# Three background matrix-vector blocks per pair of items in the up stages of a two-layer trunk, not four

## The chip, the cores and the metric

The kernel runs as one program on one NeuronCore of a Trainium2 chip. The metric is the device time of one execution in microseconds (us): three runs before the change took 2880.12, 2875.01 and 2872.11 us, median 2875.01. A profiled execution took 2877.94 us. The engines are TensorE (PE, with PEld for its weight loads), VectorE (DVE), ScalarE (ACT), GpSimd (POOL) and SyncE (SP), whose queue issues nearly all DMAs.

## The reference

Two layers, each with a mixer (gated delta net, then retention) and a convolutional feed-forward part. Scales, shifts and gains of both parts come from a conditioning vector `e` by a matrix-vector product with `ada_w`.

```python
e = jax.nn.silu(c @ cond_w + cond_b)
for i in range(DEPTH):
    mod = (e @ ada_w[i] + ada_b[i])[:, None, :]
    sh1, sc1, g1, sh2, sc2, g2 = jnp.split(mod, 6, axis=-1)
    y = mixers[i % N_MIXERS](x * (1.0 + sc1) + sh1)
    x = layer_norm(DN_ALPHA * x + (1.0 + g1) * y, ln_g[i, 0], ln_b[i, 0])
    y = conv_ffn(x * (1.0 + sc2) + sh2, ffn_up[i], ffn_conv_w[i], ffn_conv_b[i], ffn_down[i])
    x = layer_norm(DN_ALPHA * x + (1.0 + g2) * y, ln_g[i, 1], ln_b[i, 1])

def conv_ffn(h, w_up, conv_w, conv_b, w_down):
    gate, up = jnp.split(h @ w_up, 2, axis=-1)
    gate = causal_dwconv(gate, conv_w) + conv_b
    return (jax.nn.silu(gate) * up) @ w_down
```

D is 1024, the sequence 1024, the feed-forward width 2816, all in 32-bit floats; `ada_w` is 2 x 1024 x 6144.

## The kernel before, in words

**Matrix products.** Each operand is split into a high part (a copy by ACT to a reduced type, L89) and a low part (a subtraction by DVE, L90), and each product is three matmuls (L110 to L112, or L301 to L303 in the down projection). PE therefore needs a block's copy, then its low half, before the block's first matmul. The large products use Strassen's scheme in Winograd's form, seven block products in place of eight.

**Up stage** (`strassen`, called at L1781 for the feed-forward part of each layer). It runs 22 items. Items 2fp and 2fp+1 are a pair (`pair_items`): the even one makes 2 x 128 gate columns, the odd one the up columns that belong to them. From item 2 on, each is done by `wino` (L1357): two 512 KB weight loads (L1361, L1362), sums of their halves (`psub`, L1350), seven products, and a `sink` that takes each result. The sink of a gate item adds parts into `g` (L1726); then `conv_q` (L1735 to L1741) runs the convolution on DVE and ends with Silu on ACT. The sink of an up item adds and multiplies (L1762, L1763), stores the result to `ad` in DRAM (L1752), and POOL makes and stores the four combinations that the down projection reads (L1771).

**Background work.** A queue `bg` holds units of the matrix-vector product with `ada_w`. One unit (`bg_ada`) covers 512 columns and 256 rows: it issues one 512 KB load, tile `mvw` (L227, on SP's queue), and at the following step does two products on DVE (L237 or L239). A vector of 1024 columns is eight units, and every fourth unit ends in four transposes on PE (L249) and four copies on ACT. `bg_step` pops the work that is due and issues one new unit. Layer 0's up stage starts with four vectors of layer 1 in the queue (32 units), layer 1's with one (8 units). `wino` calls `bg_step` twice per item, once after the fourth product and once at the end, but not while `late` work is pending at its start (`early`), which holds for items 2 and 3. Units left over when the stage ends stay in the queue; the next loop that calls `bg_step` takes them. The tile that a unit's load goes to is set by `bg_tag[0]`: "lane" (4 buffers) within the up stage, "wr" (2 buffers) after it (L1423).

**Down stage** (`proj_gen`, L1433). Seven products, each over eleven steps j. A step's `ops` (L1482) loads the stationary block (`ar`, from `ad`, L1429), splits it into `ab`, and splits a weight block (`Bw`, `Br`, L1462) into `bb`. The tile of `ab` rotates through ("wl", "hTb", "wr") in the first five products, so that steps 2, 5 and 8 of the first one take a "wr" buffer. Each step ends in `bg_step` (L1651).

**What sets the order.** Instructions of one engine run in the order that a scheduler has given them from the code, its tile pools and its own estimates; each engine's order is fixed when the program is built. A second call of `strassen` serves retention (`direct=True`).

Of the kernel before, what the change touches and what calls it, by code (L numbers as in the profile page):

```python
# [33 lines left out]
def trunk_kernel(ctx: ExitStack, tc, A):  # L34
# [11 lines left out]
    def tl(tag, shape, dt=F32, name=None):  # L46
        return sb.tile(shape, dt, tag=tag, name=name or tag, bufs=BUFS[tag])
# [34 lines left out]
    def hs(half):  # L82
        return slice(half * HALF, (half + 1) * HALF)
# [35 lines left out]
    def bg_step(tile=mm_tile):  # L119
        bg_ps[0] = tile  # L120
        for p in pend:
            p[0] -= 1
        while pend and (pend[0][0] <= 0 or not bg):
            pend.pop(0)[1]()
            if not bg:
                break
        if bg:
            nxt = bg.pop(0)()
            if nxt:
                pend.append(list(nxt))  # L130
# [3 lines left out]
    def row_step():  # L134
        if rowp:
            rowp.pop()()
        if rowq:
            nxt = rowq.pop(0)()
            if nxt:
                rowp.append(nxt[1])  # L140
# [1149 lines left out]
    def strassen(hT0, xts, scale, shift, items, tags=("hTb", "hTb", "qkv", "qkv", "aux"), direct=False, late=()):  # L1290
# [39 lines left out]
        def block(src):  # L1330
            n = nblk[0]
            nblk[0] += 1
            t = tl(("wh", "wl")[n % 2], [P, 2, HALF], F32R, name="wb")
            split(t[:, 0], t[:, 1], src)
            return kn(t[:, 0]), kn(t[:, 1])

        def prod(src, b, onto=None, w=None):
            w = w or block(src)
            if onto is None:
                nacc[0] += 1  # L1340
                acc = (acc_tile, acc_tile, sc_tile)[nacc[0] % 3]()
            else:
                acc = onto
            for k in range(4):
                mm3(acc, w, k, B[b][k], onto is None and k == 0, k == 3, mm_on if onto is not None else pe.matmul)
            return acc

        def psub(x, y, op=ALU.subtract):
            t = mm_tile()
            dve.tensor_tensor(t, x, y, op)  # L1350
            return t

        def drain(n):
            for _ in range(min(n, len(late))):
                late.pop(0)()

        def wino(n, sink):  # L1357
            ua, ub = items[n][:2]
            early = bool(late)
            wa, wb = tl("wr", [P, D]), tl("wr", [P, D])  # L1360
            sp.dma_start(wa, ua)  # L1361
            anchor["wi"] = sp.dma_start(wb, ub)  # L1362
            a11, a12, a21, a22 = wa[:, hs(0)], wa[:, hs(1)], wb[:, hs(0)], wb[:, hs(1)]
            def copy_of(X, tag="cv"):
                t = tl(tag, [P, 516] if tag == "cv" else [P, HALF], name="pc")[:, 0:HALF]
                act.activation(t, X, AF.Copy)  # L1366
                return t

            X = prod(a11, "11")
            p1 = copy_of(X)  # L1370
            s1 = psub(a21, a22, ALU.add)
            sink(0, prod(a12, "21"), p1)
            s2 = psub(s1, a11)
            Z = prod(s1, "T1")
            z5 = copy_of(Z)
            w2 = block(s2)
            s4 = psub(a12, s2)
            drain(2)
            prod(None, "T2", X, w2)
            u2 = copy_of(X)  # L1380
            s3 = psub(a11, a21)
            drain(2)
            prod(s4, "22", Z)
            sink(1, Z, u2)
            if not early:
                bg_step()
            drain(2)
            prod(s3, "T3", X)
            u3 = copy_of(X, "t2")
            sink(3, X, z5)  # L1390
            drain(2)
            sink(2, prod(a22, "T4"), u3)
            if not early:
                bg_step()
            if n > 4:
                row_step()
# [20 lines left out]
        for n in range(2, len(items)):  # L1417
            wino(n, items[n][2]())
            if n > 2:
                drain(len(late))  # L1420
            if items[n][3]:
                items[n][3]()
# [754 lines left out]
```

## Time and profile before

| what | us |
|---|---|
| median of three runs | 2875.01 |
| profiled execution | 2877.94 |
| its span in the trace | 2876.1 |
| up stage of layer 0 (L1296 and L110 to L112) | about 847 to 1164 |
| first matmul of layer 0's down stage (L301) | 1164.69 |
| up stage of layer 1 | about 2300 to 2660 |

The mean granted clock of TensorE is 0.992. The span is the time from the first to the last instruction that the profiler recorded; the profiled time lies 1.8 us above it. A row of the timeline has its start, its length, the engine, the line, the operation and, in brackets, how long the engine stood idle before it and for what.

### The profile page before, as it was taken

Reading aid. Unit: us, or ns where it says so; the run is one execution under the profiler, and the core shown is the slowest. Engines: PE = TensorE matmul, PEld = TensorE weight load, DVE = VectorE, ACT = ScalarE, POOL = GpSimd, SP = SyncE. Lnnn points to the kernel's source line nnn. Section 1 sums busy time; section 2 is a strip of 40 time slices with the busy share of each in tenths; the row PEclk is TensorE's granted clock in tenths of the full one; section 3 lists DMA queues with packets and bytes.
Section 4 is the critical chain, followed back from the end, with each engine's and each line's share of the span. In section 5 each row is a group of like instructions: output and inputs, shape, how many; then the busy total and the mean of one; then the engine's idle time right before and its main releaser. Section 6 shows DMA issues by size and latency. Waiting matters only on the chain.

```text
span 2876.1 us, 38922 instructions
## 1 busy us (share of the span) xinstructions
PE 2787.3 (97%) x13594; PEld 2279.0 (79%) x13594; DVE 2181.4 (76%) x3874; ACT 1296.6 (45%) x2387; POOL 488.7 (17%) x517
## 2 busy tenths in 40 slices
PE   8999999999999999999999999999999999999997
PEld 6788878887787878887888887777777788888886
DVE  5788778676788878778687666666789887777869
ACT  4664465343654444546333332222344644445443
POOL 0311321000023233000000002333301033332001
PEclk9999999999999999999999999999999999999999
DMA  7233232174254655845343364665854153444843
GB/s 278 85 99 122 92 132 96 63 245 147 96 186 159 204 179 176 323 136 181 125 147 113 125 198 157 201 191 173 261 199 148 67 202 133 143 136 163 321 149 117
DMA packets 251988, 465.30 MB, mean 162 GB/s; under 512 B 24144, under 2 KB 76752, under 8 KB 251792
## 3 DMA queue, kind: packets, MB, share of 16 engines
q1 hardware_dynamic: 217472, 407.50, 42.7%
q10 hardware_dynamic: 31488, 46.15, 4.4%
q0 software_dynamic: 2832, 9.18, 0.8%
q8 instruction: 107, 1.75, 0.3%
q14 instruction: 89, 0.73, 0.1%
HBM read 346.86 MB, written 115.87 MB: 161 GB/s over the span
## 4 chain that ended last, share of the span: by engine, by line
PE 64%; DVE 16%; DMA 10%; ACT 5%; issue 4%; POOL 1%; SPq 0%; ACTq 0%; DVEq 0%; POOLq 0%
PE acc L716 10%; PE acc L1296 7%; PE acc L110 5%; PE acc L111 5%; PE acc L112 5%; PE acc L1592 4%; PE sc L716 4%; PE sc L1296 4%; PE mm L716 2%; DMA mvw<-in_ada_w 2%; PE sc L110 2%; PE sc L112 2%; PE sc L111 2%; DVE o L1740 2%; DMA wr<-in_ffn_up 1%
## 5 line engine op out<-in xcount | busy, mean ns | idle before, releaser
L716 PE MATMUL acc<-hT,wh 128*128 128x512 f32 x960 | 299.8, 394 | 0.0
L1592 PE MATMUL acc<-bb,ab 128*128 128x512 f32 x984 | 231.6, 394 | 6.5 <-DVE ab L90 5.3
L89 ACT ACTIVATE ab<-ar 128x512 fp32r<-128x512 f32 x210 | 130.9, 629 | 216.3 <-PE mm L303 56.7
L1592 PEld LDWEIGHTS acc<-bb,ab 128*128 128x128 f32 x984 | 184.0, 189 | 48.9 <-DVE ab L90 4.6
L716 PEld LDWEIGHTS acc<-hT,wh 128*128 128x128 f32 x960 | 182.3, 190 | 35.6
L1296 PE MATMUL acc<-T,wb 128*128 128x512 f32 x840 | 202.0, 389 | 0.4 <-DVE wb L90 0.4
L89 ACT ACTIVATE wb<-mm 128x512 fp32r<-128x512 f32 x216 | 124.3, 597 | 170.6 <-DVE mm L1350 155.3
L90 DVE TENSOR_TENSOR ab<-ar,ab 128x512 fp32r<-128x512 f32 x210 | 148.0, 712 | 69.6 <-ACT ab L89 68.9
L716 PE MATMUL acc<-hT,wl 128*128 128x512 f32 x480 | 196.6, 410 | 2.1 <-ACT sq L509 2.1
L1296 PEld LDWEIGHTS acc<-T,wb 128*128 128x128 f32 x840 | 157.5, 188 | 33.8 <-ACT o L1741 1.2
L90 DVE TENSOR_TENSOR wl<-wr,wh 128x1024 fp32r<-128x1024 f32 x98 | 121.4, 1239 | 76.6 <-ACT wh L89 72.7
L90 DVE TENSOR_TENSOR wb<-wr,wb 128x512 fp32r<-128x512 f32 x162 | 116.2, 719 | 65.8 <-ACT wb L89 65.7
L89 ACT ACTIVATE wh<-wr 128x1024 fp32r<-128x1024 f32 x98 | 103.8, 1060 | 127.9 <-PE acc L716 59.6
L1771 POOL TENSOR_TENSOR o<-o 128x512 f32<-128x512 f32 x80 | 113.0, 1421 | 268.6 <-DVE o L1763 130.8
L1740 DVE SCALAR_TENSOR_TENSOR o<-g,vc,o 128x512 f32<-128x512 f32 (+2 forms) x176 | 147.3, 846 | 7.1 <-ACT o L1735 5.9
L90 DVE TENSOR_TENSOR wb<-mm,wb 128x512 fp32r<-128x512 f32 x216 | 144.4, 680 | 7.3 <-ACT wb L89 7.3
L89 ACT ACTIVATE wb<-wr 128x512 fp32r<-128x512 f32 x162 | 101.2, 626 | 91.8 <-PE acc L1296 26.5
L1350 DVE TENSOR_TENSOR mm<-wr 128x512 f32<-128x512 f32 x108 | 84.9, 786 | 73.1 <-DMA wr<-in_ffn_up 59.8
L716 PE MATMUL acc<-wh,hT 128*128 128x512 f32 x384 | 134.3, 412 | 1.8 <-DVE vv L90 1.8
L1366 ACT ACTIVATE pc<-acc 128x512 f32<-128x512 f32 x143 | 84.4, 590 | 110.7 <-PE acc L1296 63.9
L239 DVE SCALAR_TENSOR_TENSOR ada<-mvw,e,ada 128x512 f32<-128x512 f32 x140 | 105.3, 752 | 24.5 <-DMA mvw<-in_ada_w 24.2
L110 PE MATMUL acc<-T,wb 128*128 128x512 f32 x292 | 114.4, 392 | 4.6 <-DVE wb L90 4.6
(677 smaller groups left out, 7350.9 us busy)
## 6 DMA issues: line engine op xcount, KB each, us to landing
wr<-in_ffn_up SPq DMA_DIRECT2D x92, 512.0 KB, 3.9
mvw<-in_ada_w SPq DMA_DIRECT2D x80, 512.0 KB, 4.3
ad<-o SPq DMA_DIRECT2D x154, 256.0 KB, 2.3
ar<-ad SPq DMA_DIRECT2D x154, 256.0 KB, 4.6
Br<-in_ffn_down SPq DMA_DIRECT2D x88, 256.0 KB, 5.2
wr<-in_ret_wv SPq DMA_DIRECT2D x32, 512.0 KB, 3.7
ar<-od SPq DMA_DIRECT2D x56, 256.0 KB, 4.2
wr<-in_gdn_wqkv SPq DMA_DIRECT2D x24, 512.0 KB, 3.5
```

Source lines behind the costliest of these rows:

```text
L89: anchor["sp"] = act.activation(dst_h, src, AF.Copy)
L90: eng.tensor_tensor(dst_l, src, dst_h, ALU.subtract)
L110: mm(acc, wl[:, k], hl[0], start=first, stop=False)
L111: mm(acc, wh[:, k], hl[1], start=False, stop=False)
L112: mm(acc, wh[:, k], hl[0], start=False, stop=last)
L239: dve.scalar_tensor_tensor(a, wr[:, kk], e[:, k:k + 1], a, ALU.mult, ALU.add)
L716: pq(pe.matmul(out, lhsT, rhs, start=start, stop=stop), cost or COST[out.shape[-1]])
L1296: return pe.matmul(*a, skip_group_check=True, **kw)
L1350: dve.tensor_tensor(t, x, y, op)
L1592: return pe.matmul(*args, skip_group_check=True, **kw)
L1740: dve.scalar_tensor_tensor(tv, gv[:, c0 - j:c1 - j], w[:, 2 - j:3 - j], tv, ALU.mult, ALU.add)
L1771: (dve if fp == 0 else pool).tensor_tensor(o[d], o[x], o[y], op)
```

## The change

The first of the two calls of `bg_step` in `wino` is now made only in items with an even number (those with gate columns), and in the retention call as before. The second one, at the item's end, stays.

```diff
             prod(s4, "22", Z)
             sink(1, Z, u2)
-            if not early:
+            if not early and (n % 2 == 0 or direct):
                 bg_step()
             drain(2)
             prod(s3, "T3", X)
...
             sink(2, prod(a22, "T4"), u3)
             if not early:
                 bg_step()
```

For items 4 to 21 of an up stage this is 27 steps, not 36. In layer 0 the queue of 32 units is then not empty at the stage's end: five are issued by the steps of the down stage.

The rows of DVE (line, operation, output and inputs) in the up item of pair 8/9 of layer 0's up stage, before; `ada<-mvw` are a unit's two products, L1350 the sums of weight halves, the first of them needing the second weight load:

```order
L90 TENSOR_TENSOR wb<-wr,wb 128x512 x2
L1350 TENSOR_TENSOR mm<-wr 128x512
L253 SCALAR_TENSOR_TENSOR v_8007<-cs,vc 128x4
L237 TENSOR_SCALAR ada<-mvw,e 128x512
L1350 TENSOR_TENSOR mm<-mm,wr 128x512
L274 TENSOR_TENSOR fs_12000<-v_8007,vc 128x8
L275 TENSOR_TENSOR fh_12001<-v_8007,vc 128x8
L1726 TENSOR_TENSOR g<-acc,pc 128x512
L239 SCALAR_TENSOR_TENSOR ada<-mvw,e,ada 128x512
L90 TENSOR_TENSOR wb<-wr,wb 128x512
L1740 SCALAR_TENSOR_TENSOR o<-g,vc,o 128x512 x2
```

and now:

```order
L1740 SCALAR_TENSOR_TENSOR o<-g,vc,o 128x511
L239 SCALAR_TENSOR_TENSOR ada<-mvw,e,ada 128x512
L1740 SCALAR_TENSOR_TENSOR o<-g,vc,o 128x510
L239 SCALAR_TENSOR_TENSOR ada<-mvw,e,ada 128x512
L90 TENSOR_TENSOR wb<-wr,wb 128x512 x2
L1726 TENSOR_TENSOR g<-acc,pc 128x512
L1350 TENSOR_TENSOR mm<-wr 128x512
L90 TENSOR_TENSOR wb<-wr,wb 128x512
L1350 TENSOR_TENSOR mm<-mm,wr 128x512
L1740 SCALAR_TENSOR_TENSOR o<-g,vc,o 128x512 x2
```

The two products have moved from behind the first L1350 to ahead of it.

SP's queue at the end of layer 0's up stage, before (names with their numbers; `ad0` is the store of gated columns, `ar` its reload, `Bw` the weights):

```order
L1462 DMA Bw_10628<-in_ffn_down 128x512 x2
L1462 DMA Bw_10631<-in_ffn_down 128x512
L1752 DMA ad0_6815<-o_10456 128x512
L1429 DMA ar_10637<-ad0_6815 128x512
L1462 DMA Bw_10631<-in_ffn_down 128x512
L1429 DMA ar_10658<-ad0_6815 128x512
```

and now, with a second piece from a few rows later, where the third and the fourth of the five units stand:

```order
L1462 DMA Bw_10582<-in_ffn_down 128x512 x2
L1462 DMA Bw_10585<-in_ffn_down 128x512
L227 DMA mvw_10614<-in_ada_w 128x2x512
L1752 DMA ad0_6815<-o_10406 128x512
L227 DMA mvw_10652<-in_ada_w 128x2x512
L1429 DMA ar_10591<-ad0_6815 128x512
L1462 DMA Bw_10585<-in_ffn_down 128x512
L1429 DMA ar_10616<-ad0_6815 128x512
```

```order
L1429 DMA ar_10831<-ad0_6815 128x512
L1462 DMA Br_10839<-in_ffn_down 128x512
L1752 DMA ad0_6815<-o_10421 128x512
L227 DMA mvw_10678<-in_ada_w 128x2x512
L1429 DMA ar_10841<-ad0_6815 128x512
L1462 DMA Br_10849<-in_ffn_down 128x512
L227 DMA mvw_10704<-in_ada_w 128x2x512
L1429 DMA ar_10883<-ad0_6815 128x512
```

Four of the five loads now stand between the stores and reloads with which the down stage begins; the fifth follows.

DVE at the low half of step 5 of the first down product, before (`ab_10746` is that step's stationary tile):

```order
L90 TENSOR_TENSOR bb_10771<-Bw_10709,bb_10771 128x512
L90 TENSOR_TENSOR ab_10725<-ar_10723,ab_10725 128x512
L90 TENSOR_TENSOR bb_10728<-Bw_10666,bb_10728 128x512
L90 TENSOR_TENSOR bb_10749<-Bw_10666,bb_10749 128x512
L90 TENSOR_TENSOR ab_10746<-ar_10744,ab_10746 128x512
L90 TENSOR_TENSOR ab_10768<-ar_10766,ab_10768 128x512
```

and now (`ab_10733` is that of step 5):

```order
L90 TENSOR_TENSOR ab_10833<-ar_10831,ab_10833 128x512
L239 SCALAR_TENSOR_TENSOR ada_10675<-mvw_10678,e_154,ada_10675 128x512 x2
L90 TENSOR_TENSOR ab_10843<-ar_10841,ab_10843 128x512
L90 TENSOR_TENSOR bb_10846<-Bw_10795,bb_10846 128x512
L90 TENSOR_TENSOR bb_10888<-Br_10817,bb_10888 128x512
L239 SCALAR_TENSOR_TENSOR ada_10675<-mvw_10704,e_154,ada_10675 128x512 x2
L90 TENSOR_TENSOR ab_10733<-ar_10731,ab_10733 128x512
```

The products of two of the moved units stand among the low halves, and step 5's low half comes behind those of other steps and behind both products of `mvw_10704`.

## The prediction

> **What bounds the kernel now.** I read the engine totals and the chain that ended last first, then windows over the stages that the diff can reach, then what TensorE (PE) waited for in them.
>
> ```profile
> PE 2787.3 (97%) x13594; PEld 2279.0 (79%) x13594; DVE 2181.4 (76%) x3874; ACT 1296.6 (45%) x2387; POOL 488.7 (17%) x517
> PE 64%; DVE 16%; DMA 10%; ACT 5%; issue 4%; POOL 1%; SPq 0%; ACTq 0%; DVEq 0%; POOLq 0%
> ```
>
> PE is busy in 97% of the span. VectorE (DVE) work taken out is worth only the PE idle time that it causes, and a new PE wait is paid in full. The windows (columns: length, then busy us and instructions of PE, PEld, DVE, ACT, POOL, then clock, DMA share, GB/s) cover the up stage of layer 0 and that of layer 1.
>
> ```profile
> 847.00:1164.00 317.00, 311.06 (x1371) 253.04 (x1370) 262.53 (x405) 148.48 (x303) 96.33 (x77) 1.00 0.53 179
> 2300.00:2660.00 360.00, 360.00 (x1585) 296.94 (x1584) 281.24 (x414) 168.42 (x286) 109.06 (x86) 1.00 0.46 155
> ```
>
> Layer 1's up stage has no idle PE at all; its queue holds 8 units, so the change only stretches them over more items. I cost it at nothing: DVE is busy 281 of 360 us there, and nobody waits for the units. Layer 0's stage idles 317.00 − 311.06 = 5.94 us, and the waits of PE in that window name the cause:
>
> ```profile
> PE acc L110 <- DVE wb L90: 4.6, 4, 1.6
> PE sc L110 <- DVE wb L90: 1.3, 1, 1.3
> ```
>
> Five waits, 5.9 us, all for the low half of a weight block. That is all that the up stage can give back. One of them, around 913 us, in the timeline:
>
> ```profile
> 898.16 0.33 SPq L1362 DMA_DIRECT2D wr<-in_ffn_up  x1
> 903.73 0.70 DVE L1350 TENSOR_TENSOR mm<-wr 128x512 f32<-128x512 f32 x1 [3.66 <-DMA wr<-in_ffn_up]
> 906.66 1.29 DVE L239 SCALAR_TENSOR_TENSOR ada<-mvw,e,ada 128x512 f32<-128x512 f32 x1
> 908.48 1.52 DVE L1740 SCALAR_TENSOR_TENSOR o<-g,vc,o 128x512 f32<-128x512 f32 x2
> 910.04 0.72 ACT L1741 ACTIVATE o<-o,vc 128x512 f32<-128x512 f32 x1 [2.49 <-DVE o L1740]
> 911.14 1.08 ACT L89 ACTIVATE wb<-mm 128x512 fp32r<-128x512 f32 x2
> 912.48 1.28 DVE L90 TENSOR_TENSOR wb<-mm,wb 128x512 fp32r<-128x512 f32 x2
> 913.22 0.50 PE L110 MATMUL acc<-T,wb 128*128 128x512 f32 x1 [1.30 <-DVE wb L90]
> ```
>
> DVE waits 3.66 us for the item's second weight load, then does the sum of L1350, a unit's two products (the second is shown), and convolution steps; ACT's Silu waits for these and stands ahead of the copy that makes the block; PE comes 1.30 us too soon. The unit is one piece of that pile.
>
> **The change, part by part.** *Up stage, layer 0.* Items 4 to 21 are nine pairs; before they take 9 × 4 = 36 steps, after 9 × 3 = 27, while the queue holds 4 vectors × 8 = 32 units. Prices of one unit's work, from the instruction groups:
>
> ```profile
> L239 DVE SCALAR_TENSOR_TENSOR ada<-mvw,e,ada x140: 734/743/1296, 89.6 to 2378.4; 128x512 f32<-128x512 f32 x140
> L237 DVE TENSOR_SCALAR ada<-mvw,e x20: 475/480/487, 88.5 to 2357.7; 128x512 f32<-128x512 f32 x20
> L249 PE MATMUL mm<-cst,ada x32: 271/272/273, 857.2 to 1137.3; 128*128 128x128 f32 x32
> ```
>
> So a unit is 2 × 0.74 = 1.5 us of DVE at the median, every fourth ends in 4 × 0.27 = 1.1 us of PE, and each loads 512 KB. Five units leave the up stage: 7.4 us of DVE work, none of it on PE's path except through the five waits. How much of 5.9 us goes? By the order of the changed kernel, the waiting item of pairs 8/9, 10/11 and 16/17 gets the matrix-vector work ahead of the weight wait, where DVE idled 3.66 us (as in pair 4/5, which has no wait now). Those pairs' waits are 1.30, 0.50 and 1.60 us: 3.4 us saved. Pairs 6/7 and 14/15 get a third order with the steps still between: kept. Pairs 12/13 and 20/21 keep the order of those that wait, and the last now does matrix-vector work there that it lacked: one wait of a mean size, 5.9/7 = 0.84 us, added. Sum −2.5 us; bounds 0 (the waits stay) and −5.9 (all go).
>
> *Down stage, layer 0.* The five units are not dropped. They run at the steps of the first product of the down projection, L1651, with the tile tag "wr". Each issues its load on SP's queue and, one step later, its two products on DVE. The end of the up stage looks like this:
>
> ```profile
> 1159.90 0.33 SPq L1429 DMA_DIRECT2D ar<-ad  x1
> 1173.32 0.32 SPq L1429 DMA_DIRECT2D ar<-ad  x1
> 1162.64 0.63 ACT L89 ACTIVATE ab<-ar 128x512 fp32r<-128x512 f32 x1 [4.78 <-DMA ar<-ad]
> 1164.69 0.39 PE L301 MATMUL acc<-bb,ab 128*128 128x512 f32 x1
> 1178.57 0.63 ACT L89 ACTIVATE ab<-ar 128x512 fp32r<-128x512 f32 x1 [0.69 <-DMA ar<-ad]
> 1178.94 0.39 PE L301 MATMUL acc<-bb,ab 128*128 128x512 f32 x1
> ```
>
> Between the first and the last `ar` issue stand 11 such loads, 10 weight loads and one store on SP: 22 pieces of 256 KB, 5.77 MB. Step 0 starts on PE at 1164.69 and step 5 at 1178.94, each step some 2.85 us. ACT is already waiting for `ar` transfers here, which the transfers' rate explains:
>
> ```profile
> 1160.00:1166.00 6.00, 6.00 (x28) 4.99 (x27) 1.52 (x3) 1.00 (x2) 0.00 (x0) 1.00 0.72 238
> 1166.00:1180.00 14.00, 13.65 (x60) 10.97 (x60) 13.71 (x19) 11.50 (x22) 5.31 (x4) 1.00 1.04 389
> 1180.00:1190.00 10.00, 10.00 (x46) 8.29 (x45) 8.84 (x13) 3.71 (x7) 1.07 (x1) 1.00 1.05 394
> ```
>
> From 1166 on the DMA engines are full (share 1.04). DVE is full as well (13.71 of 14). This is the one stretch of the stage without room, and the moved units land in it.
>
> What is late next is told by the tile tag. The stationary tile of steps 2, 5 and 8 is also a "wr" tile, of two buffers. In the new order of SP the fourth moved load (`mvw_10704`) takes the buffer that step 2 frees, and the stationary tile of step 5 (`ab_10733`) the same buffer after it. So on DVE `ab_10733` stands right behind the two products of `mvw_10704`, and these wait for a load that is behind 11 `ar`, 11 weight loads, 5 stores and two other moved loads: with its own two, 33 pieces, 8.65 MB. Behind DVE's waiting products are queued all later low halves, and PE needs `ab_10733` for step 5.
>
> When does it land? Data from 1160: 6 × 238 = 1.43 MB by 1166, plus 14 × 389 = 5.45, so 6.87 by 1180. Before, the load issued at 1173.32 has 5.77 MB up to its end, and the copy that waits for it starts at 1178.57; by then 1.43 + 12.57 × 0.389 = 6.32 MB have moved: pieces behind it share the engines, some 0.5 MB. In the same way the moved load lands at 8.65 + 0.5 = 9.15 MB, (9.15 − 6.87)/0.394 = 5.8 us after 1180, at 1185.8. Then its two products 1.5, the copy 0.63, the low half 0.69: 1188.6. Step 5 started at 1178.94, and 1188.6 − 1178.94 = 9.7, so **PE waits about 9.5 us** in the sum. (If the up stage ends sooner by what it gains, this queue starts sooner with it.) Bounds: with no sharing it lands at its own 8.65 MB, at 1184.5, and if two of the five stores come behind it, at 8.13 MB, at 1183.2; with the same 2.8 us after that the wait is 7. For the upper end the fifth load shares too, 0.52 MB or 1.3 us, and one pair of operands (1.2 us) stands ahead on the full DVE: 12.
>
> [...]
>
> The rest I cost at nothing, with its cover: the transposes of the first moved unit (1.1 us on PE, moved from the up stage to just before step 0, not added); the gate work and POOL's, whose order doesn't change; the last moved unit's products, which DVE meets after step 5 and which are covered by the eager operands of steps 6 and 7, unless the wait of step 5 has used these up (then up to 3 us, in a rival).
>
> **Sum.** −2.5 + 9.5 = +7. The profiled execution took 2877.94 us (span 2876.1), so 2884.9; it stands 2.9 us above the median of the runs, 2875.01, so the same sum there gives **2882.0**.
>
> **Rivals**, each against 2875.0:
>
> 1. *The forecast*: the net of wait and gain, from 7 − 5.9 = +1.1 to 12 − 0 = +12: 2876 to 2887, likeliest 2882. For it: one tile ring, in-order DVE, full DMA engines. Chance 0.55.
> 2. *The load comes in time.* If SP issues it early, as its buffer is free once step 2 is done (1164.69 + 3 × 2.85 = 1173), it could land after the 5.3 us of the median `ar` transfer below, at 1178.3; with the 2.8 us behind it PE waits 2.2 us. That 33 pieces cannot have moved by then speaks against it. With the up stage's −2.5 to −5.9 the net is −0.3 to −3.7: 2871 to 2875. Chance 0.12.
> 3. *It waits twice, and the kernel is slower.* The fifth load (`mvw_10729`) lands one more unit behind; its products block DVE again with low halves of steps 8 to 10 behind them. It decides if PE has used up the operands made ahead, which a first wait makes likely. A second 3 us with the upper bound of the first: 12 + 3 − 0 = +15, and +12 with less: 2887 to 2890. Chance 0.23.
> 4. *Nothing measurable.* The up stage keeps its waits (each has convolution and Silu in its pile too), and the weight loads of the down stage run far enough ahead to feed PE: within 3 us, 2872 to 2878. Chance 0.10.
>
> ```profile
> ar<-ad SPq DMA_DIRECT2D x13, 256.0 KB, 5.3
> ```
>
> **How the numbers follow.** 0.3%, 8.6 us, is what a measurement of this kernel tells from no change: below 2866.4 is faster, above 2883.6 slower. Case 1 puts about a third (0.18) above that and 0.37 within; case 3 all 0.23 above; cases 2 and 4 lie within but for 0.02, if the up stage's idle goes and something gives 3 us more that I don't see. So faster 0.02, same 0.57, slower 0.41. The range runs from 2873, which leaves out the lower half of case 2 (0.06) and the lowest part of case 4 (0.02), to 2889, which leaves out the upper half of case 3 (0.12).
>
> **What would show it.** Right: PE idle of 7 to 12 us before step 5 of layer 0's first down product, released by DVE's L90 of `ab`, with `mvw` as what DVE itself waited for; up-stage idle down from 5.9 to about 3.5 us; layer 1 unchanged. Wrong: no idle at step 5 (case 2), or a second one before step 8 (case 3), or up-stage waits in the same pairs as before (case 4). A planner that issues the moved loads later than the order shows would break the sum at the landing time.

## The result and the profile after

The changed kernel takes 2888.47 us (median of five runs, 2887.21 to 2895.28) against 2875.01 us of the kernel before (five runs, 2871.49 to 2880.12). The ratio is 1.0056, 95% interval 1.0045 to 1.0067: slower by 13 to 19 us. The profiled execution has a span of 2886.4 us at a clock of 0.992.

Windows over the stretches that the prediction showed of before (columns as there: length, busy us and instructions of PE, PEld, DVE, ACT, POOL, then clock, DMA share, GB/s):

```profile
847.00:1164.00 317.00, 310.53 (x1370) 253.43 (x1368) 257.36 (x392) 146.31 (x286) 95.02 (x76) 1.00 0.52 175
1166.00:1180.00 14.00, 13.50 (x57) 10.18 (x56) 14.00 (x22) 9.11 (x23) 6.54 (x4) 1.00 1.02 387
1180.00:1190.00 10.00, 1.89 (x5) 1.51 (x6) 6.73 (x11) 2.93 (x5) 1.75 (x1) 0.65 1.05 388
2300.00:2660.00 360.00, 358.35 (x1572) 294.43 (x1572) 279.44 (x413) 166.49 (x282) 104.45 (x84) 1.00 0.44 147
```

The third row is the loss: PE works 1.89 us of ten, where it worked all ten before, while the DMA engines are as full as before, at 388 GB/s. The fourth has lost the full 360.00 of PE. The first is hardly changed, although the units' work has left it.

The place itself, from the timelines of SP, of DVE with one row of ACT, and of PE (`...` marks rows left out):

```profile
1175.96 0.38 SPq L227 DMA_DIRECT2D mvw<-in_ada_w  x1
1177.92 0.38 SPq L227 DMA_DIRECT2D mvw<-in_ada_w  x1
```

```profile
1181.87 1.54 DVE L239 SCALAR_TENSOR_TENSOR ada<-mvw,e,ada 128x512 f32<-128x512 f32 x2 [1.25 <-DMA mvw<-in_ada_w]
...
1185.14 1.53 DVE L239 SCALAR_TENSOR_TENSOR ada<-mvw,e,ada 128x512 f32<-128x512 f32 x2
1186.70 0.63 ACT L89 ACTIVATE ab<-ar 128x512 fp32r<-128x512 f32 x1 [2.54 <-DVE ada L239]
1187.36 0.69 DVE L90 TENSOR_TENSOR ab<-ar,ab 128x512 fp32r<-128x512 f32 x1 [0.70 <-ACT ab L89]
```

```profile
1165.02 0.50 PE L301 MATMUL acc<-bb,ab 128*128 128x512 f32 x1 [1.73 <-DVE ab L90]
...
1179.48 0.39 PE L303 MATMUL acc<-bb,ab 128*128 128x512 f32 x1
1188.11 0.80 PE L301 MATMUL acc<-bb,ab 128*128 128x512 f32 x1 [8.24 <-DVE ab L90]
1188.70 0.63 PE L302 MATMUL acc<-bb,ab 128*128 128x512 f32 x1
...
1193.34 0.39 PE L301 MATMUL acc<-bb,ab 128*128 128x512 f32 x1
```

The load of the fourth moved unit is issued at 1177.92 and lands 6.6 us later, at 1184.5. DVE, which had waited 1.25 us for the third unit's load, comes to its two products at 1185.14. ACT's copy of step 5 has waited 2.54 us for these products: it writes the buffer that they read. The copy starts at 1186.70, the low half of step 5 at 1187.36, and PE starts step 5 at 1188.11 after 8.24 us of waiting. Two things there were in no term of the sum: a wait of 1.73 us already at step 0, and the speed after the long wait. The 12 matmuls of step 5 take 1193.34 − 1188.11 = 5.23 us; at the 0.227 us that separates two of them elsewhere in this product it would be 2.72. The clock column of the third window, 0.65, says the same, and over the slow stretch alone the granted clock is a half:

```profile
1183.10:1193.20 10.10, 5.09 (x12) 4.03 (x13) 4.92 (x8) 2.32 (x5) 0.00 (x0) 0.50 1.05 390
```

In the up stage of layer 0 the sum of waits barely moved (5.9 us before, in five waits), since a new one came in:

```profile
PE acc L110 <- DVE wb L90: 4.3, 3, 2.4
PE sc L110 <- DVE wb L90: 1.5, 2, 1.2
```

The longest, 2.4 us, has no counterpart before. DVE and then PE at that place, item 14:

```profile
1018.62 0.75 DVE L239 SCALAR_TENSOR_TENSOR ada<-mvw,e,ada 128x512 f32<-128x512 f32 x1 [4.18 <-DMA mvw<-in_ada_w]
1019.29 0.68 DVE L90 TENSOR_TENSOR wb<-wr,wb 128x512 fp32r<-128x512 f32 x1
```

```profile
1020.03 0.50 PE L110 MATMUL acc<-T,wb 128*128 128x512 f32 x1 [2.38 <-DVE wb L90]
```

As at step 5, a unit's product stands ahead of a block's low half on DVE; here the product itself waits 4.18 us for its load, and the low half waits behind it.

In layer 1's up stage PE waits once, where it did not wait before:

```profile
PE sc L110 <- DVE wb L90: 1.6, 1, 1.6
```

Where the time lies, by the start of the first matmul of each stage in the two profiles (the difference is after less before, of the stretch that begins there):

| stretch begins with | before, us | after, us | stretch longer by |
|---|---|---|---|
| up stage, layer 0 (its start) | 747.75 | 747.76 | +0.3 (1.7 of it the wait at step 0) |
| first down product, layer 0 | 1164.69 | 1165.02 | +11.9 |
| its second product, then the rest up to layer 1's up stage | 1195.26 | 1207.44 | −5.2 |
| up stage, layer 1 | 2244.92 | 2251.94 | +2.5 |
| first down product, layer 1 | 2651.05 | 2660.53 | +0.8 |
| its second product, to the end | 2680.97 | 2691.21 | +0.0 |

The −5.2 belongs to no edit of the change. The first experiment below leaves everything ahead of layer 1's up stage as it was before, and that same stretch took 1043.8 us in it, against 1049.7 in the profile of before and 1044.5 in that of after; over the thirteen profiles here it takes 1043.8 to 1049.7, so the profile of before happened to be slow there. Without that row the sum is 15.4 us, within the 13 to 19 of the timed runs.

The other rows, too, come from one profile on each side. In six of them the units of layer 1's up stage are as before (in one of these moved, not left out), and that stage takes 405.9 to 406.8 us; in seven of them the step is left out there, and it takes 408.6 to 413.1. The +2.5 is thus the low end of a loss of 2 to 7 us. The +0.8 of the next row is in the changed kernel's profile alone: the other six with that step left out take 29.9 to 30.2 us there, against 29.9 before, so it is chance.

### The profile page after: what moved, and what is told of

It reads as the page before. It is cut to its first block, busy times and chain, and to the rows that moved or that the text cites. A ratio compares the mean times of both kernels' runs of the same rounds, so it can differ in the third digit from the quotient of the medians.

```text
span 2886.4 us, 38896 instructions
## 1 busy us (share of the span) xinstructions
PE 2785.4 (97%) x13594; PEld 2277.9 (79%) x13594; DVE 2180.6 (76%) x3874; ACT 1299.1 (45%) x2387; POOL 487.8 (17%) x517
## 4 chain that ended last, share of the span: by engine, by line
PE 70%; DVE 13%; DMA 9%; ACT 4%; issue 3%; POOL 1%; SPq 0%; ACTq 0%; DVEq 0%; POOLq 0%
PE acc L716 13%; PE acc L1296 8%; PE acc L110 5%; PE acc L111 5%; PE acc L112 5%; PE sc L1296 4%; PE sc L716 4%; PE acc L1592 4%; PE mm L716 2%; DMA mvw<-in_ada_w 2%; PE sc L110 2%; PE sc L111 2%; PE sc L112 2%; PE mm L1592 1%; PE sc L1592 1%
## 5 line engine op out<-in xcount | busy, mean ns | idle before, releaser
L1740 DVE SCALAR_TENSOR_TENSOR o<-g,vc,o 128x512 f32<-128x512 f32 (+2 forms) x176 | 154.4, 887 | 7.7 <-ACT o L1735 6.4
L1350 DVE TENSOR_TENSOR mm<-wr 128x512 f32<-128x512 f32 x108 | 81.6, 756 | 68.4 <-DMA wr<-in_ffn_up 56.6
```

What stands on the lines that cost most here:

```text
L1740: dve.scalar_tensor_tensor(tv, gv[:, c0 - j:c1 - j], w[:, 2 - j:3 - j], tv, ALU.mult, ALU.add)
```

## The experiments

Theory A was that the loss is the five moved units in layer 0's down stage, by way of the tile ring and the order on DVE. Its rivals were: small reorderings everywhere (B), and the bytes alone (C).

**Layer 1 alone.** Layer 0 as before; `far[0]` is true in layer 1's feed-forward part.

```diff
-            if not early and (n % 2 == 0 or direct):
+            if not early and (n % 2 == 0 or direct or not far[0]):
```

> The first step of odd items is left out in layer 1's up stage only; layer 0 is as before. Theory A (the loss is five matrix-vector units moved into layer 0's down stage, whose loads share the two-buffer tile ring with the stationary tile of step 5, on an in-order DVE): no wait of PE at step 5, layer 0's stages as before within 1 us, and only the +2.5 us that the changed kernel lost in layer 1's up stage: 2874 to 2881. Rival B (the loss is spread over small reorderings everywhere): half of the loss or more stays, 2882 to 2889.

2874.01 us, ratio 1.0001 (0.9988 to 1.0014). The first down product of layer 0 takes 30.5 us (1162.46 to 1192.94), as before. Layer 1's up stage is 2.7 us longer (408.8 against 406.1), with these waits of PE in 2290 to 2660, where before has none:

```profile
PE sc L110 <- DVE wb L90: 1.9, 2, 1.6
```

So B falls for the large part, and the prediction's zero for layer 1 was wrong by 2.7 us in this profile; the interval of the timed runs is too wide to show these by itself.

**Another tile for the moved loads.**

```diff
-        bg_tag[0] = "wr"
+        bg_tag[0] = "wr" if direct else "lane"
```

> The changed kernel, but the five units' loads in layer 0's down stage go to the four-buffer ring lane, not to the two-buffer ring wr that the stationary tiles of steps 2, 5 and 8 use. Same five loads, 2.6 MB, same DVE work, in the same 30 us. Theory A (ring): the loads need not wait for step 2 and four of them go out before the first reload; step 0 then waits longer than the 1.7 us of the changed kernel, some 4 us, step 5 waits less than 2 us and TensorE's clock does not drop there; first product 30.6 + 2 us or less after its first matmul, where the changed kernel has 42.4; time some 6 us below the changed kernel, 2880 to 2884. Rival C (bytes: 2.6 MB more on full DMA engines, 6.7 us at 0.39 MB/us plus the slow clock, whichever tile takes them): the waits of steps 0 to 5 add up to the same 10 to 12 us, time within 2 us of the changed kernel.

2884.11 us, ratio 1.0031 (1.0019 to 1.0043). With free buffers, four of the loads went out ahead of the first reload. All waits of PE from 1160 to 1200, and the first of them:

```profile
PE acc L301 <- DVE ab L90: 3.4, 2, 3.2
```

```profile
1166.69 0.79 PE L301 MATMUL acc<-bb,ab 128*128 128x512 f32 x1 [3.23 <-DVE ab L90]
1167.28 0.63 PE L302 MATMUL acc<-bb,ab 128*128 128x512 f32 x1
```

Same bytes, same stretch, and the waits fall from 1.7 + 8.2 to 3.4 us: the product takes 32.8 us, not 42.4. C is refuted as the main cause. What is left here is the 3.2 us at step 0, with a slow clock behind it (0.63 us rows); that the bytes of the four loads cause it is supported by the next run, in which no moved load goes out ahead of the first reload and step 0 does not wait.

**From step 5 on, in the same ring.**

```diff
-                bg_step()
+                if gate or p > 0 or j >= 5:
+                    bg_step()
```

> The changed kernel, but the down stage of layer 0 calls the background step only from step 5 of the first product on; the tile ring stays wr. Theory A (ring): step 5 has no wait, but the load of the second unit now stands in the ring ahead of the stationary tile of step 8, whose low half follows that unit's products on DVE: by position some 44 pieces of 256 KB, 11.5 MB, landing near 1193, so PE waits 6 to 10 us at step 8 and the clock drops there; time like the changed kernel, 2885 to 2890. Rival C (bytes): three or four of the loads now come after the operands of steps 5 to 8 are loaded, so the waits sum to less than 4 us and the time is 2877 to 2882.

2892.04 us, ratio 1.0062 (1.0044 to 1.0080). Step 5 has no wait; step 8 has it, and the second product waits 2.0 us more, which puts the time above the 2890 expected. DVE, then PE at step 8:

```profile
1192.97 0.49 DVE L237 TENSOR_SCALAR ada<-mvw,e 128x512 f32<-128x512 f32 x1 [2.10 <-DMA mvw<-in_ada_w]
1193.50 0.75 DVE L239 SCALAR_TENSOR_TENSOR ada<-mvw,e,ada 128x512 f32<-128x512 f32 x1
1194.94 0.69 DVE L90 TENSOR_TENSOR ab<-ar,ab 128x512 fp32r<-128x512 f32 x1 [0.69 <-ACT ab L89]
```

```profile
1195.69 0.80 PE L301 MATMUL acc<-bb,ab 128*128 128x512 f32 x1 [9.05 <-DVE ab L90]
```

The wait went where the ring says, to the next stationary tile that shares a buffer with a unit, and the landing time worked out from bytes (1193) is the 1192.97 of the trace. Having the units later helped nothing while they shared that ring.

**Later, and in the other ring.** As the last two together, with each load tied behind the newest reload that is already issued (`after("a")`):

```diff
-            sp.dma_start(wr, A["ada_w"][...])
+            with after("a" if bg_late[0] else None):
+                sp.dma_start(wr, A["ada_w"][...])
```

> The changed kernel, but the five units start from step 5 of the first down product, in the ring lane, and each load is tied behind the newest reload already issued, so that on SP they stand between the reloads of steps 5 to 10. Theory A (ring and order): nothing on PE's path waits for them; first product 30.6 to 31.5 us, waits in it under 1 us, clock kept; what stays is the changed up stages (layer 0 about -2, layer 1 about +2.5): 2873 to 2879. Rival C (bytes): the 2.6 MB still go through full DMA engines before step 10's operands, so waits of 4 to 7 us at steps 8 to 10: 2880 to 2884.

> As the run before it, with layer 1's up stage as in the kernel before the change. Theory A: layer 1's item-7-to-8 step of some +3 us is gone; 2870 to 2876, that is the same as before or a little faster. Rival: layer 1's +3 us belongs to chance order and stays.

The first of these takes 2879.47 us, ratio 1.0009 (0.9996 to 1.0022), the second 2876.10 us, ratio 1.0004 (0.9989 to 1.0018). The first down product takes 32.3 and 32.2 us, a little above the 31.5 that was expected, and all waits of PE in it, in the first of the two kernels (from 1163 to 1196), are

```profile
PE acc L303 <- DVE ab L90: 0.6, 2, 0.5
PE acc L304 <- DVE bb L90: 0.4, 1, 0.4
```

With layer 1 as before, its up stage takes 405.9 us, 0.2 less than before; with the step left out there (the first of the two) 411.7. The loss in layer 1 comes from the left-out steps in layer 1. So with ring, early loads and layer 1 taken away, the whole loss is gone, and nothing is gained either: layer 0's up stage takes 417.6 us in both, as 416.9 before.

**Keeping PE busy in the wait.** 36 extra matmuls, their results unused, between steps 4 and 5:

```diff
+                    if not gate and not final and p == 0 and j == 5:
+                        scr = sc_tile()
+                        for _ in range(36):
+                            pe.matmul(scr, warm[0][0][:, 0:P], warm[1][0], start=True, stop=True)
+                    warm = (a, w)
```

> The changed kernel with 36 extra matmuls (results unused) issued on PE between steps 4 and 5 of layer 0's first down product, where PE sat idle for 8.2 us. Theory D (the slow clock behind the wait is due to PE's idling): the 12 matmuls of step 5 start every 0.23 us, not every 0.43 us, the first product takes 40.0 to 40.8 us, not 42.4, and the time falls by some 2 us. Rival E (the slow start has another cause, such as operands that arrive late): they stay at 0.43 us and the product takes 42 us or more.

PE at step 5, where L1644 are the extra matmuls (31 of them came to stand there, five two steps earlier):

```profile
1181.81 7.19 PE L1644 MATMUL sc<-bb,ab 128*128 128x512 f32 x31
1188.84 0.39 PE L301 MATMUL acc<-bb,ab 128*128 128x512 f32 x1
1189.06 0.39 PE L302 MATMUL acc<-bb,ab 128*128 128x512 f32 x1
```

Step 5 starts hardly sooner (22.9 us after step 0, not 23.1), but its matmuls follow each other by 0.23 us, at a granted clock of 1.00, and the product takes 39.6 us, not 42.4, a little less than the 40.0 to 40.8 expected. So the 2.5 us of slow pace are due to PE's idling. The timed run, 2888.88 us, ratio 1.0046 (1.0032 to 1.0060), does not resolve them: its up stages happened to be 1.5 and 4.5 us longer than those of the changed kernel.

**Fewer left-out steps.** Four kernels that leave nothing for the down stage, or nearly so. First, the step left out in items 5, 7 and 9 only:

```diff
-            if not early and (n % 2 == 0 or direct):
+            if not early and (n % 2 == 0 or direct or n > 9):
```

> The first step of odd items is left out only in items 5, 7 and 9 of each up stage: 33 steps for 32 units, none left for the down stage. Theory A: no wait in layer 0's down stage; the up stage of layer 0 gains 0 to 2 us, that of layer 1 loses 0 to 2.5: 2872 to 2880. Rival B (small reorderings): above 2882 in spite of no unit being left over.

2889.59 us, ratio 1.0052 (1.0036 to 1.0067): a miss, and the time that rival B named for it. The first down product is as before, 30.9 us, but the up stage of layer 0 takes 426.3 us, not 416.9. So a changed order in the up stage can cost this much by itself, though in the changed kernel, with 417.3 us there, it did not. Waits of PE from 845 to 1170:

```profile
PE acc L110 <- DVE wb L90: 7.7, 7, 1.6
PE sc L110 <- DVE wb L90: 5.0, 4, 1.6
PE sc L1296 <- ACT pc L1366: 1.2, 1, 1.2
```

Twelve waits, not five, ten of them in items 11 to 21, which had their four steps per pair as before. What differs there is which unit falls on which step: three left-out steps shift it by three places of the four after which transposes follow. That this makes the waits is a guess (theory F in the texts below). So the next runs varied the number of left-out steps (in layer 0 alone), `n > 11`, `n > 5` and `n > 7` in place of `n > 9`:

> Layer 0's up stage alone leaves out the first step of items 5, 7, 9 and 11: four steps, a multiple of the four units that end in transposes, so that from item 12 on the units fall on the same places of a pair as before the change. Theory F (the place of a unit in the pair decides whether DVE's products stand behind or ahead of the waits): up stage 415 to 419 us, where three left-out steps gave 426.3 and none 416.9; time 2871 to 2879. Rival G (each left-out step adds its share of the 9.4 us): up stage near 429, time above 2884.

> Layer 0's up stage leaves out the first step of item 5 alone, so the units shift by one of four places for the rest of the stage. Theory F: a third order, whose waits I can't derive; its late rows are like those of the changed kernel's pairs with and without waits in turn, so 413 to 420 us. Rival G: 416.9 + 9.4/3 = 420 or more.

> Layer 0's up stage leaves out the first step of items 5 and 7, a shift by two places. Theory F: its late pairs have the row order that three left-out steps have in items 14 to 17, where both items of a pair wait 1.4 to 1.7 us, so 420 to 427 us, time 2877 to 2886. Rival G: 416.9 + 2 x 9.4/3 = 423, time 2881; this run alone tells little, together with the other two it does.

| left out in layer 0 | up stage, us | first down product, us | time, us | ratio, 95% interval |
|---|---|---|---|---|
| none | 416.9 | 30.6 | 2873.74 to 2875.01 | |
| one | 423.0 | 29.9 | 2878.71 | 1.0023 (1.0014 to 1.0032) |
| two | 425.0 | 30.1 | 2881.38 | 1.0035 (1.0019 to 1.0052) |
| three (both layers) | 426.3 | 30.9 | 2889.59 | 1.0052 (1.0036 to 1.0067) |
| four | 418.2 | 31.0 | 2878.43 | 1.0018 (1.0006 to 1.0029) |
| nine (the change) | 417.3 | 42.4 | 2888.47 | 1.0056 (1.0045 to 1.0067) |

The times were not all taken on one chip; each ratio is against runs of the kernel before on the same one. Four gives almost the stage of none, which a share per step (429, rival G) does not: G falls. That the place of a unit in the pair decides fits this, but is not shown: one left-out step missed theory F's range (413 to 420) by 3 us and fits G's, and the timed runs do not tell four (2878.43) from one (2878.71). The waits of four, from 830 to 1163:

```profile
PE sc L110 <- DVE wb L90: 3.1, 4, 1.4
PE acc L110 <- DVE wb L90: 2.8, 3, 1.5
PE acc L301 <- DVE ab L90: 0.7, 1, 0.7
```

5.9 us in the up stage, the size of before. Of its 4.7 us over the kernel before in the timed runs, the two stages of its profile show 1.3 + 0.5. With one left-out step PE waits 10.7 us for low halves from 845 to 1167, in seven waits, the longest of 2.28 us at 1031.19 and of 3.12 us at 1112.14; behind the second, matmuls come 0.43 us apart until 1115.75.

**Moved, not removed.** The step of odd items goes to the end of even ones, 36 steps as before:

```diff
             if not early:
                 bg_step()
+                if n % 2 == 0 and not direct:
+                    bg_step()
```

> The first step of odd items is not left out but made at the end of even items, behind their own last step: 36 steps as before, 32 units, none left over. Theory A: no loss in the down stage; what the up stages do depends on where the units fall against DVE's waits for the second weight load: layer 0 up stage 382 to 386 us, time 2870 to 2880. Rival B (any change of order in the up stage costs some 10 us): up stage above 390, time above 2882.

2875.70 us, ratio 1.0001 (0.9987 to 1.0015), layer 0's up stage 416.3 us, layer 1's 406.5. The 382 to 386 us expected are too short for the stage as the table counts it; counted from the matmul before which PE waits for 1.05 us (780.26 before, 774.48 here) it is 384.4 us before and 383.8 here. A change of order in the up stage need not cost, and this one does not pay. None of the kernels tried is measurably faster than the kernel before.

## Why the prediction was right and wrong

**Step 5 of the down product: right in mechanism and place, and near in time.** The load was to land at 1185.8, its products to follow at once and PE to start at 1188.6. It landed at 1184.5, its products started at 1185.14, behind other low halves on DVE, and PE started at 1188.11: the landing came 1.3 us sooner than the sum, and DVE's queue, in no term of it, took half of that back, so the near agreement is in part luck. The wait of 8.24 us lies within the bounds of 7 to 12. ACT's 2.54 us of waiting for the products show the ring at work. The run from step 5 on confirms ring and order, since the wait moved to step 8; the run with the other tile confirms that the bytes alone are not it. The second wait of rival 3 did not come: behind step 5 no wait of PE before the second product is above 0.2 us.

**The price of a long wait: a term that was missing.** The sum counted the wait and no more. Behind it 12 matmuls ran at about half speed, 5.23 us in place of 2.72, and the run with a busy PE shows that the idling is the cause. From 1188.70 to 1192.97 the trace has ten intervals of 0.427 us. The clock also dropped behind shorter waits, one of 1.79 us among them (last section). The profile of before could have given such a term: behind a wait of PE of 2.11 us, up to 2089.29, matmuls come 0.43 us apart from 2090.48 to 2093.04, and the granted clock from 2090.2 to 2093.5 is 0.50. As an estimate from that stretch, 3.3 us at half pace would have been a term of 1.7 us; behind step 5 the trace was slow for 5.2 us.

**Step 0: "the rest I cost at nothing" failed.** Two of the moved loads stand ahead of the first reload, 1.05 MB, and the prediction counted these bytes for step 5 but not for step 0. The first reload, issued at 1158.52, landed after 5.0 us; before, issued at 1159.90, it took 2.6. PE waited 1.73 us for step 0, 3.23 us where four loads stood ahead, and not at all where none did (the runs from step 5 on).

**The up stage of layer 0: the −2.5 is not shown.** In the changed kernel's profile the stage takes 417.26 − 1.73 = 415.53 us up to the wait at step 0, against 416.94: −1.4. But the other five kernels with the same steps left out there take 415.4 to 418.0 us, less any wait at step 0, and the run of layer 1 alone, with the stage as before, 416.4: no gain stands clear of this scatter. The pairs came out mostly as the rows said: no wait any more in pairs 8/9 and 16/17 and 0.26 in 10/11, and 6/7 and 14/15 kept theirs (1.21 and 1.62 us). The step that failed took the products ahead of the weight wait as free: in item 14 one of them had its own load to wait for, and PE paid 2.38 us. The page of after shows such waits over the whole kernel (last column: idle time of DVE ahead of the group), first before, then after:

```profile
L239 DVE SCALAR_TENSOR_TENSOR ada<-mvw,e,ada 128x512 f32<-128x512 f32 x140 | 105.3, 752 | 24.5 <-DMA mvw<-in_ada_w 24.2
```

```profile
L239 DVE SCALAR_TENSOR_TENSOR ada<-mvw,e,ada 128x512 f32<-128x512 f32 x140 | 104.3, 745 | 43.8 <-DMA mvw<-in_ada_w 43.3
```

DVE does the same work and waits 19 us more for the units' loads.

**The up stage of layer 1: 0 became +2.5 or more.** "Nobody waits for the units" was true of before. The reason given, DVE's 281 of 360 us, is an average and says nothing on who stands behind a unit in the order. The run of layer 1 alone gives +2.7, and taking that part away (the second of the late runs) gives −0.2; over all profiles the loss is 2 to 7 us.

**In all**, 15.4 us by the stages of one profile against the +7 of the sum: wait 8.2 (9.5 in the sum), clock 2.5, step 0 1.7, small waits and the last transposes in the first product 1.1, layer 0's up stage −1.4 (−2.5), layer 1 2.5 + 0.8. The sign of the sum was right, but by its own line of 2883.6 us the prediction gave "slower" 0.41 and "same" 0.57. That 2888.47 lies just under the upper end of the range, in the 2887 to 2890 of rival 3, is luck: rival 3's second wait did not come. The size was half of what came, for terms set to nothing (clock, step 0, layer 1), not for the main one.

## What to carry to other kernels

Work that is put off by a counter does not vanish: find the loop that takes it next, and see which tile ring and which in-order queue it shares there with the operands of the critical engine. Look whether the load of a small piece of background work has landed when its turn comes on an in-order engine: what it holds up are the instructions queued behind it, not its own duration (in item 14 a product of 0.75 us waited 4.18 us for its load, and PE 2.38 us for the low half behind it). And dropping a fraction of periodic work changes the order of what is left: with one to three steps left out, one stage here grew by 6.0 to 9.4 us and with four by 1.3, so several counts are worth a look before one is judged.

## What was not expected of the hardware

The length of a wait does not by itself tell whether PE is slow behind it. With the other tile a wait of 3.23 us was enough: the matmuls behind it were 0.43 us apart from 1167.28 to 1169.41, and the granted clock in these five us was 0.66:

```profile
1166.00:1171.00 5.00, 4.31 (x12) 3.20 (x12) 4.28 (x5) 3.71 (x14) 2.89 (x2) 0.66 1.03 375
```

In the run of layer 1 alone one of 2.24 us in the up stage was enough:

```profile
990.06 0.79 PE L110 MATMUL sc<-T,wb 128*128 128x512 f32 x1 [2.24 <-DVE wb L90]
990.64 0.63 PE L111 MATMUL sc<-T,wb 128*128 128x512 f32 x1
```

The eight matmuls there take 3.53 us, 1.7 us more than at 0.227 us each, at a granted clock of 0.50. In the second of the late runs a wait of 1.79 us (until 872.66) was followed by the same, from 873.96 on. In the changed kernel's up stage, waits of 1.21, 1.62 and 2.38 us were followed by one matmul of 0.50 us and then by the usual pace. What decides between these cases no run here tests.

Also, profiles of code that is the same up to layer 1's up stage differ by up to 6 us in the stretch between the two feed-forward stages (1049.7, 1043.8). The slower of the two has a clock of 0.50 there from 1363.2 to 1366.5 and from 2090.2 to 2093.5, the other none; at 1.7 us each, an estimate from the eight matmuls above, that is 3.4 of the 5.9 us. A stage has to be compared with its own start, not by the end of the span, and in more than one profile.
